# Recurrence gates as pairs of 64-row matmuls, joined by transfers, and a last output in halves

## The chip, the cores and the metric

The kernel runs on one core of a Trainium2 chip. The metric is the device time of one execution in microseconds (us). The engines are TensorE (PE, with its weight loads listed as PEld), VectorE (DVE), ScalarE (ACT), GpSimd (POOL) and SyncE (SP). Each works through its own queue in order. SP issues nearly all loads and stores, POOL a few.

## The reference, cut to what matters

One layer of an encoder over 512 tokens of 1024 features, in float32: a SwiGLU block, a mixer, a second SwiGLU block, each added to x. The mixer sums a gated linear recurrence (forward and backward) and a windowed attention. The change concerns the gates of the recurrence and the end of the second SwiGLU block:

```python
def _rglru_scan(xc, w_gates, b_gates, lam):          # called once for each direction
    xb = xc.reshape(B_, S, LRU_BLOCKS, LRU_BLOCK)    # 16 blocks of 64 features
    gates = jnp.einsum('bsni,gnio->gbsno', xb, w_gates)   # one 64x64 matrix per gate and block
    gates = gates.reshape(2, B_, S, W) + b_gates[:, None, None, :]
    r = jax.nn.sigmoid(gates[0])
    i = jax.nn.sigmoid(gates[1])
    log_a = -LRU_C * r * jax.nn.softplus(-lam)
    a = jnp.exp(log_a)
    bx = jnp.sqrt(-jnp.expm1(2.0 * log_a)) * (i * xc)
    _, h = lax.associative_scan(_lin_combine, (a, bx), axis=1)
    return h
...
xc = _centred_dwconv(xr, conv_w[l], conv_b[l])
y_lru = (h_fwd + h_bwd) * jax.nn.gelu(gr)
...
x = x + FFN_RES * _swiglu(_rmsnorm(x, norm_ffn2[l]), w_ffn2_gu[l], w_ffn2_down[l])   # the output
```

The gate matrices are block diagonal: a gate of 128 features is two independent 64x64 products.

## The kernel before, in words

Features lie on the 128 partitions, the 512 tokens along the free dimension; a "tile" f is 128 features x 512 tokens, so x has 8 tiles. Every float32 product is made of three matmuls on operands cut into a high and a low part: high x high, high x low, low x high (`mm3`, lines 144 to 147). `load_w` loads a weight chunk of up to 128x1024 through SP into one of three buffers `wraw` and cuts it into `wh` (a copy on ACT, L118) and `wl` (a subtraction on DVE, L121), four buffers each. A chunk of 1024 columns gives 24 matmuls over 512 tokens.

PSUM has two pools of four tiles of 128x512: `acc` for the large products, `aux` for the recurrence's gates, the attention and other small products. SBUF tiles of 128x512 come from a pool of 48 (`big_t`), pairs of them from a pool of four (`pair_t`).

The order on each queue is not written out by hand: a scheduler places each instruction by the program's order and its own estimates of durations, so that independent matmuls fill a wait. `after(i, prev)` adds an order by hand, `high_priority` puts evictions and weight cuts forward.

The stages, by the trace: first SwiGLU block to about 352 us; projection `xr` with the convolution, eight chunks, one per tile f; projections q, k, v for two halves of the heads, twelve chunks each (phases `t0`, `t1`); the gate branches, 24 chunks (`g`); the output projection; from about 800 us the second SwiGLU block, whose last products leave eight output tiles through `out2`.

The recurrence and the attention have no stage of their own. They are generators in two lanes, and after each chunk `weave(RATE[...])` runs some of their steps: for the recurrence four per chunk in `xr`, three in `t0`, two in `t1`, three in `g`. The recurrence's generator `lru(fs)` is entered twice, for tiles 0 to 3 once all four are convolved, and for tiles 4 to 7. For each tile it loads the gate matrices (128 x 512, zeros off the two diagonal blocks), cuts the convolved tile `xc` into `ch` and `cl`, and for each of two directions and two gates runs three matmuls of 128 rows (L145 to L147), evicts by a sigmoid on ACT (L606), multiplies the second gate by `xc` on DVE (L611) and takes a tanh of the first on ACT (L613). After four tiles come all exponentials (L618), all square roots (L623) and the scans on DVE (L631, L633); the groups stand together because ACT loads a table when the function changes.

In the second block's last products (`ffn`, from L416), the four outputs of a half are accumulated together until the last six of 22 steps k, which are run output by output; each output is then scaled (L442) and added to x (L901) on DVE and stored by SP (L902).

In the attention, `scores` (L744) already runs pairs of 64-row matmuls: for each of three products, one head on the upper and one on the lower 64 partitions, 256 columns each, into two PSUM tiles (L757).

Of the kernel before, what the change touches and what calls it, by code (L numbers as in the profile page):

```python
# [11 lines left out]
AF = mybir.ActivationFunctionType  # L12
ALU = mybir.AluOpType
# [3 lines left out]
P = 128  # L17
T = 512
# [49 lines left out]
def block_kernel(ctx: ExitStack, tc, a, out):  # L68
# [18 lines left out]
    def big_t(dt=F32, shape=(P, T), n="b"):  # L87
        return big.tile(list(shape), dt, tag="big", bufs=NBIG, name=nm(n))
# [7 lines left out]
    def aux_t():  # L96
        return aux.tile([P, T], F32, tag="aux", name=nm("aux"))
# [43 lines left out]
            split(raw[:, s], H[:, s], L[:, s], act)  # L141
        return H, L

    def mm3(ps, wh, wl, xh, xl, first, last):
        nc.tensor.matmul(ps, wh, xh, start=first, stop=False)  # L145
        nc.tensor.matmul(ps, wh, xl, start=False, stop=False)  # L146
        nc.tensor.matmul(ps, wl, xh, start=False, stop=last)  # L147

    def feat_chunk(src, nk, xh, xl, ps, k0, ktot, act=True):
        H, L = load_w(src, nk * P, act)  # L150
# [45 lines left out]
        nc.scalar.activation(r, ps, AF.Copy)  # L196
        return r, rcol, vx

    def after(i, prev):

        i, prev = getattr(i, "ins", i), getattr(prev, "ins", prev)
        tc.add_manual_dep(i, prev.name, mybir.DependencyInfo(
            mybir.DependencyClass.NoSync, mybir.DependencyReason.DATA), reason="order")


    mark = {}
# [127 lines left out]
    def ffn(wgu, ws, wd, xh, xl, S, ssum, plain, res, emit_out, lead=None):  # L334
        hs = []
        r = None
        pre = {}
# [78 lines left out]
        for q in range(2):  # L416
            outs = range(q * 4, q * 4 + 4)
            for i in range(2):
                t = pair_t()
                for m in range(2):  # L420
                    nc.sync.dma_start(t[:, m], res(q * 4 + i * 2 + m))
                    xres[q * 4 + i * 2 + m] = t[:, m]
            ps = [aux_t() if q == 0 else acc_t() for _ in outs]
            ws_ = []

            def put_in(i, k):
                H, L = ws_[k // 2]
                c = slice((k % 2) * T + i * P, (k % 2) * T + (i + 1) * P)
                mm3(ps[i], H[:, c], L[:, c], *cuts[q, k], k == 0, k == FT - 1)
# [8 lines left out]
            for i, m in enumerate(outs):  # L438
                for k in range(FT - 2 * DTAIL, FT):
                    put_in(i, k)  # L440
                t = big_t(n="dn")
                nc.vector.scalar_tensor_tensor(t, ps[i], -0.5, r, ALU.mult, ALU.mult)  # L442
                emit_out(m, t)


    lanes = {"lru": [], "att": []}
# [131 lines left out]
        xc[f] = y  # L578


    last_act = [None]

    def lru(fs):
        un = []
        cuts = {}

        def cut(f):
            if f in fs:
                cuts[f] = big_t(F32R, n="ch"), big_t(F32R, n="cl")
                split(xc[f], *cuts[f])  # L590

        cut(fs[0])
        for f in fs:
            gH, gL = load_w(a["wgate"][f], T)
            cut(f + 1)
            cH, cL = cuts.pop(f)
            yield
            for d in range(2):
                rt = []
                for g in range(2):  # L600
                    q = d * 2 + g
                    s = slice(q * P, (q + 1) * P)
                    ps = aux_t()
                    mm3(ps, gH[:, s], gL[:, s], cH, cL, True, True)
                    t = big_t(n="gate")
                    i = nc.scalar.activation(t, ps, AF.Sigmoid, bias=small[:, C_BG + f * 4 + q : C_BG + f * 4 + q + 1])  # L606
                    if last_act[0] is not None:
                        after(i, last_act[0])
                    rt.append(t)
                r, ix = rt  # L610
                nc.vector.tensor_tensor(ix, ix, xc[f], ALU.mult)  # L611
                th = big_t(n="th")
                tanh = nc.scalar.activation(th, r, AF.Tanh, scale=sp4[:, f * 2 + d : f * 2 + d + 1])  # L613
                un.append((f, d, r, ix, th))
                yield

        for f, d, r, ix, th in un:
            exp = nc.scalar.activation(r, r, AF.Exp, scale=sn8[:, f * 2 + d : f * 2 + d + 1])  # L618
            after(exp, tanh)
            nc.vector.scalar_tensor_tensor(ix, r, 1.0, ix, ALU.add, ALU.mult)  # L620
            yield
        for f, d, av, ix, th in un:
            last_act[0] = nc.scalar.activation(th, th, AF.Sqrt)  # L623
            after(last_act[0], exp)
            nc.vector.tensor_tensor(ix, ix, th, ALU.mult)
            yield
        h = None
        for f, d, av, ix, th in un:
            if d == 0:
                h = th  # L630
                nc.vector.tensor_tensor_scan(h, av, ix, 0.0, ALU.mult, ALU.add)  # L631
            else:
                nc.vector.tensor_tensor_scan(th[:, ::-1], av[:, ::-1], ix[:, ::-1], 0.0, ALU.mult, ALU.add)  # L633
                nc.vector.tensor_tensor(h, h, th, ALU.add)
                A[f] = h
            yield


# [14 lines left out]

    V = {}
# [246 lines left out]
        nc.vector.tensor_tensor(o, ps, xres[m], ALU.add)  # L901
        nc.sync.dma_start(out[m], o)  # L902

    ffn(a["w2gu"], a["w2s"], a["w2d"], xh, xl, forms.S, ssum, NPLAIN[1], lambda m: xd[m], out2)


def layouts(inp):
# [28 lines left out]
    bd = np.zeros((KT, P, 4, P), wg.dtype)  # L936
    for b in range(16):
        s = slice((b % 2) * 64, (b % 2) * 64 + 64)
        bd[b // 2, s, :, s] = wg[:, :, b].reshape(4, 64, 64).transpose(1, 0, 2)
    o["wgate"] = bd.reshape(KT, P, 4 * P)  # L940
    col = lambda v: np.asarray(v).reshape(-1, KT, P).transpose(2, 1, 0).reshape(P, -1)
    o["small"] = con(np.concatenate([
        col(f("norm_ffn1")[0]), col(f("norm_mix")[0]), col(f("norm_ffn2")[0]),
        col(f("conv_w")[0]), col(f("conv_b")[0]),
        col(f("lru_b_gates")[0].reshape(4, D)), col(f("lru_lambda")[0]),
        np.tile(f("q_norm")[0], 2)[:, None], np.tile(f("k_norm")[0], 2)[:, None]], 1))


# [31 lines left out]
```

## Time and profile before

| | |
|---|---|
| median of 3 runs | 1133.14 us (1133.12 to 1133.49) |
| the profiled execution | 1133.02 us, span of the program 1130.9 us |
| granted TensorE clock | 0.999 |
| TensorE matmuls | 6872, busy 1124.3 us (99%) |
| DVE, ACT, POOL busy | 836.0, 594.7 and 19.3 us |
| loaded from HBM, written | 121.17 MB, 8.39 MB |

The span runs from the first to the last instruction; 2.1 us of the execution lie around it. A row of a timeline gives start, duration, engine, line, operation, output<-inputs, shape and count; successive matmuls overlap in the pipeline, so their cost is the distance between starts. A row of grouped instructions ends with the busy time and mean duration in ns, then the idle time of the engine just ahead of them and what ended it. A row of waits gives who waited for whom, the sum in us, the count and the longest.

### The profile page before, as it was taken

Reading aid. Unit: us, or ns where it says so; the run is one execution under the profiler, and the core shown is the slowest. Engines: PE = TensorE matmul, PEld = TensorE weight load, DVE = VectorE, ACT = ScalarE, POOL = GpSimd, SP = SyncE. Lnnn points to the kernel's source line nnn. Section 1 sums busy time; section 2 is a strip of 40 time slices with the busy share of each in tenths; the row PEclk is TensorE's granted clock in tenths of the full one; section 3 lists DMA queues with packets and bytes.
Section 4 is the critical chain, followed back from the end, with each engine's and each line's share of the span. In section 5 each row is a group of like instructions: output and inputs, shape, how many; then the busy total and the mean of one; then the engine's idle time right before and its main releaser. Section 6 shows DMA issues by size and latency. Waiting matters only on the chain.

```text
span 1130.9 us, 17246 instructions
## 1 busy us (share of the span) xinstructions
PE 1124.3 (99%) x6872; PEld 995.1 (88%) x6872; DVE 836.0 (74%) x1288; ACT 594.7 (53%) x896; POOL 19.3 (2%) x52
## 2 busy tenths in 40 slices
PE   9999999999999999999999999999999999999998
PEld 8899999988888888888788888888999999998886
DVE  7898888884836798797855576859688888894542
ACT  8554544563624595985564254656445445464330
POOL 0000000000000000010110000000000000000000
PEclk9999999999999999999999999999999999999999
DMA  7242333443433342353443332355123233352320
GB/s 263 94 131 79 119 102 102 136 137 94 130 94 111 94 159 84 112 167 103 132 149 104 93 103 88 109 169 184 56 93 116 92 112 113 94 168 93 131 75 38
DMA packets 43553, 130.69 MB, mean 116 GB/s; under 512 B 5968, under 2 KB 8272, under 8 KB 43472
## 3 DMA queue, kind: packets, MB, share of 16 engines
q1 hardware_dynamic: 39600, 119.36, 33.8%
q0 software_dynamic: 3296, 9.97, 2.8%
q8 instruction: 54, 0.88, 0.3%
q10 hardware_dynamic: 576, 0.26, 0.1%
q14 instruction: 27, 0.22, 0.1%
HBM read 121.17 MB, written 8.39 MB: 115 GB/s over the span
## 4 chain that ended last, share of the span: by engine, by line
PE 97%; DVE 1%; ACT 1%; issue 0%; DVEq 0%
PE acc L260 29%; PE acc L145 11%; PE acc L146 11%; PE acc L147 11%; PE aux L260 5%; PE aux L145 4%; PE aux L146 4%; PE aux L147 4%; PE acc L666 4%; PE acc L665 3%; PE acc L667 3%; PE aux L784 1%; PE aux L795 1%; PE aux L757 1%; PE acc L373 1%; PE aux L373 0%
## 5 line engine op out<-in xcount | busy, mean ns | idle before, releaser
L118 ACT ACTIVATE wh<-wraw 128x1024 fp32r<-128x1024 f32 (+3 forms) x242 | 241.3, 999 | 333.9 <-PE acc L260 96.8
L121 DVE TENSOR_TENSOR wl<-wraw,wh 128x1024 fp32r<-128x1024 f32 (+3 forms) x254 | 291.4, 1150 | 138.5 <-ACT wh L118 137.9
L260 PE MATMUL acc<-s,wh 128*128 128x256 f32 x1216 | 220.6, 283 | 0.1
L260 PEld LDWEIGHTS acc<-s,wh 128*128 128x128 f32 x1216 | 189.7, 192 | 0.3 <-ACT p L317 0.3
L260 PE MATMUL acc<-s,wl 128*128 128x256 f32 x608 | 172.1, 283 | 0.0
L145 PE MATMUL acc<-xh,wh 128*128 128x512 f32 x304 | 120.2, 395 | 0.0
L146 PE MATMUL acc<-xl,wh 128*128 128x512 f32 x304 | 119.0, 392 | 0.0
L147 PE MATMUL acc<-xh,wl 128*128 128x512 f32 x304 | 118.8, 391 | 0.0
L260 PEld LDWEIGHTS acc<-s,wl 128*128 128x128 f32 x608 | 116.7, 192 | 0.0
L260 PE MATMUL acc<-xh,wl 128*128 128x256 f32 x304 | 86.0, 283 | 0.0
L260 PE MATMUL acc<-xl,wh 128*128 128x256 f32 x304 | 86.0, 283 | 0.0
L260 PE MATMUL acc<-xh,wh 128*128 128x256 f32 x304 | 86.0, 283 | 0.0
L665 PE MATMUL acc<-wh,xh 128*128 128x512 f32 x192 | 75.2, 392 | 0.0
L666 PE MATMUL acc<-wh,xl 128*128 128x512 f32 x192 | 74.8, 390 | 0.0
L667 PE MATMUL acc<-wl,xh 128*128 128x512 f32 x192 | 74.8, 389 | 0.0
L294 DVE TENSOR_TENSOR wraw<-wraw,pair 128x1024 f32<-128x1024 f32 x57 | 69.5, 1220 | 0.8
L145 PE MATMUL aux<-hh,wh 128*128 128x512 f32 x176 | 68.5, 389 | 0.0
L146 PE MATMUL aux<-hl,wh 128*128 128x512 f32 x176 | 68.5, 389 | 0.0
L147 PE MATMUL aux<-hh,wl 128*128 128x512 f32 x176 | 68.5, 389 | 0.0
L145 PE MATMUL acc<-hh,wh 128*128 128x512 f32 x176 | 68.5, 389 | 0.0
L146 PE MATMUL acc<-hl,wh 128*128 128x512 f32 x176 | 68.5, 389 | 0.0
L147 PE MATMUL acc<-hh,wl 128*128 128x512 f32 x176 | 68.5, 389 | 0.0
(194 smaller groups left out, 2197.5 us busy)
## 6 DMA issues: line engine op xcount, KB each, us to landing
wraw<-wqkv SPq DMA_DIRECT2D x24, 512.0 KB, 3.6
wraw<-wg SPq DMA_DIRECT2D x24, 512.0 KB, 3.6
wraw<-w1d SPq DMA_DIRECT2D x22, 512.0 KB, 3.6
wraw<-w2d SPq DMA_DIRECT2D x22, 512.0 KB, 3.6
pair<-w2s SPq DMA_DIRECT2D x20, 512.0 KB, 3.6
wraw<-w2s SPq DMA_DIRECT2D x20, 512.0 KB, 3.6
wraw<-w1s SPq DMA_DIRECT2D x18, 512.0 KB, 3.6
pair<-w1s SPq DMA_DIRECT2D x18, 512.0 KB, 3.6
```

The source lines that it names most:

```text
L118: nc.scalar.activation(H, raw, AF.Copy)
L121: nc.vector.tensor_tensor(L, raw, H.bitcast(F32), ALU.subtract)
L145: nc.tensor.matmul(ps, wh, xh, start=first, stop=False)
L146: nc.tensor.matmul(ps, wh, xl, start=False, stop=False)
L147: nc.tensor.matmul(ps, wl, xh, start=False, stop=last)
L260: nc.tensor.matmul(o, w_[:, c], x_, start=first and m + k == 0 and w_ is H and x_ is xh_, stop=m + k == 4 and w_ is L, skip_group_check=True)
L294: nc.vector.tensor_tensor(t, t, o, ALU.add)
L373: nc.tensor.matmul(pre[i], w[i][1][:, s], xh[k], start=k == 0, stop=False)
L665: nc.tensor.matmul(pss[j], xh[kk][:, tj], H[:, s], start=kk == 0, stop=False)
L666: nc.tensor.matmul(pss[j], xl[kk][:, tj], H[:, s], start=False, stop=False)
L667: nc.tensor.matmul(pss[j], xh[kk][:, tj], L[:, s], start=False, stop=kk == KT - 1)
L757: mm = nc.tensor.matmul(ps[hp][:, i * 256 : (i + 1) * 256], q_[o, n * P : (n + 1) * P], keys(k_[o]), start=k_ is kh and q_ is qh, stop=q_ ...
```

## The change

**Gates.** The gate matrices are stored without their zeros: 128 x 256, block b = 0 on partitions 0 to 63 and b = 1 on 64 to 127, with the columns of the two gates r and i of a direction side by side. A tile's products become 12 matmuls of 64 rows x 128 columns over 512 tokens, in six pairs (b = 0 and b = 1), into four `aux` tiles taken at once: one per direction and block, r on partitions 0 to 63 and i on 64 to 127. `after` chains the twelve, and the first of them waits, by a semaphore now, for the last sigmoid of the tile before. Four sigmoids evict into two `pair_t` tiles. Eight transfers per tile, each 64 partitions x 512 tokens, issued by POOL, put the two blocks of r together into one tile of 128 partitions, and those of i into another. The multiply by `xc` and the tanh (`use`) of a tile come during the next tile's steps.

**Steps.** There is one generator for all eight tiles, entered after tile 0's convolution instead of after tile 3's; a tile has six steps, of which the third holds its matmuls; the `xr` rate is three steps per chunk instead of four. Exponentials and square roots still come in two groups of four tiles, with a step for every two of them; the scans of the first four tiles are spread over the steps of the last four.

**Last output.** The last of the eight output tiles runs step k = 16 as before; for the last five k the products of the first 256 tokens come first, then those of the last 256, the latter into an `aux` tile. Scaling, adding and storing are done for each half.

```diff
-LRU_F = 4
+EHALF = 5
 RATE = {
-    "xr": {"lru": 4, "att": 0.0},
+    "xr": {"lru": 3, "att": 0.0},
...
+        def gates(f, W):
+            ps = [[aux_t() for _ in range(2)] for _ in range(2)]
+            X = cuts.pop(f)
+            mm = None
+            for d in range(2):
+                c = slice(d * P, (d + 1) * P)
+                for w, x in ((0, 1), (1, 0), (0, 0)):
+                    for b in range(2):
+                        o = slice(b * HD, (b + 1) * HD)
+                        prev, mm = mm, nc.tensor.matmul(
+                            ps[d][b], W[w][o, c], X[x][o], start=x == 1, stop=w + x == 0)
+                        if prev is not None:
+                            after(mm, prev)
+                        elif evicted:
+                            after(mm, evicted[-1], True)
+            for d in range(2):
+                q = C_BG + f * 4 + d * 2
+                both = pair_t()
+                for b in range(2):
+                    i = nc.scalar.activation(both[:, b], ps[d][b], AF.Sigmoid, bias=small[:, q + b : q + b + 1])
+                    if last is not None:
+                        after(i, last)
+                evicted.append(i)
+                r, ix = (big_t(n="gate") for _ in range(2))
+                for g, t in enumerate((r, ix)):
+                    for b in range(2):
+                        nc.gpsimd.dma_start(t[b * HD : (b + 1) * HD], both[g * HD : (g + 1) * HD, b])
+                got.append((f, d, r, ix))
+
+        def use():
+            f, d, r, ix = got.pop(0)
+            nc.vector.tensor_tensor(ix, ix, xc[f], ALU.mult)
+            th = big_t(n="th")
+            un.append((f, d, r, ix, th))
+            return nc.scalar.activation(th, r, AF.Tanh, scale=sp4[:, f * 2 + d : f * 2 + d + 1])
...
+            for f in fs:
+                W = load_w(a["wgate"][f], 2 * P)
+                early = len(got) > 0
+                for k in range(2):
+                    if early:
+                        tanh = use()
+                    yield
+                gates(f, W)
+                yield
+                cut(f + 1)
+                for _ in range(3):
+                    if todo:
+                        scan(*todo.pop(0))
+                    yield
...
     conv(f, ps, rb)
+        if f == 0:
+            lanes["lru"].append(lru())
     weave(RATE["xr"])
-        if (f + 1) % LRU_F == 0:
-            lanes["lru"].append(lru(range(f + 1 - LRU_F, f + 1)))
...
+        for k in range(k0, FT):
+            put_half(ps[i][:, t0], i, k, t0, False, k == FT - 1)
+        for k in range(k0, FT):
+            put_half(p2, i, k, t1, k == k0, k == FT - 1)
+        scaled(ps[i][:, t1], t1)
+        nc.vector.tensor_tensor(o[:, t1], t[:, t1], x[:, t1], ALU.add)
+        scaled(ps[i][:, t0], t0)
+        nc.vector.tensor_tensor(o[:, t0], t[:, t0], x[:, t0], ALU.add)
+        end(t0, o)
+        scaled(p2, t1)
+        nc.vector.tensor_tensor(o[:, t1], o[:, t1], t[:, t1], ALU.add)
+        end(t1, o)
```

More of the change, by code (lines that the diff above doesn't have):

```diff
@@ L142, in load_w, with mm3 @@
         return H, L
[L144 to L147, printed above, removed]
+    def mm3(ps, wh, wl, xh, xl, first, last, skip=False):
+        nc.tensor.matmul(ps, wh, xh, start=first, stop=False, skip_group_check=skip)
+        nc.tensor.matmul(ps, wh, xl, start=False, stop=False, skip_group_check=skip)
+        nc.tensor.matmul(ps, wl, xh, start=False, stop=last, skip_group_check=skip)
     def feat_chunk(src, nk, xh, xl, ps, k0, ktot, act=True):
@@ L332, in strassen, with ffn @@
         last_product(prev)
-    def ffn(wgu, ws, wd, xh, xl, S, ssum, plain, res, emit_out, lead=None):
+    def ffn(wgu, ws, wd, xh, xl, S, ssum, plain, res, emit_out, lead=None, end=None):
         hs = []
@@ L424, in ffn, with put_in, put_half @@
             ws_ = []
-            def put_in(i, k):
+            def put_in(i, k, last=FT - 1):
                 H, L = ws_[k // 2]
                 c = slice((k % 2) * T + i * P, (k % 2) * T + (i + 1) * P)
-                mm3(ps[i], H[:, c], L[:, c], *cuts[q, k], k == 0, k == FT - 1)
+                mm3(ps[i], H[:, c], L[:, c], *cuts[q, k], k == 0, k == last)
+            def put_half(o, i, k, tok, first, last):
+                H, L = ws_[k // 2]
+                c = slice((k % 2) * T + i * P, (k % 2) * T + (i + 1) * P)
+                mm3(o, H[:, c], L[:, c], *(t[:, tok] for t in cuts[q, k]), first, last, True)
             for j in range(FT // 2):
@@ L438, in ffn @@
             for i, m in enumerate(outs):
+                if end is not None and m == KT - 1:
+                    break
                 for k in range(FT - 2 * DTAIL, FT):
@@ L443, in ffn, with scaled @@
                 emit_out(m, t)
+        if end is None:
+            return
+        i, x, k0 = 3, xres[KT - 1], FT - EHALF
+        for k in range(FT - 2 * DTAIL, k0):
+            put_in(i, k, k0 - 1)
+        t, o, p2 = big_t(n="dn"), big_t(n="o"), aux_t()[:, :half]
+        t0, t1 = slice(0, half), slice(half, T)
+        def scaled(p, tok):
+            nc.vector.scalar_tensor_tensor(t[:, tok], p, -0.5, r[:, tok], ALU.mult, ALU.mult)
+        for k in range(k0, FT):
[10 more added lines that the diff above has]
+        end(t1, o)
     lanes = {"lru": [], "att": []}
@@ L578, in conv, with lru @@
         xc[f] = y
[L581 to L585, printed above, removed]
+    def lru():
+        got, evicted, cuts, last = [], [], {}, None
         def cut(f):
-            if f in fs:
+            if f < KT:
                 cuts[f] = big_t(F32R, n="ch"), big_t(F32R, n="cl")
                 split(xc[f], *cuts[f])
[L592 to L597, printed above, removed]
-            for d in range(2):
[L599 to L628, printed above, removed]
@@ L632, in lru @@
             else:
                 nc.vector.tensor_tensor_scan(th[:, ::-1], av[:, ::-1], ix[:, ::-1], 0.0, ALU.mult, ALU.add)
-                nc.vector.tensor_tensor(h, h, th, ALU.add)
-                A[f] = h
+                nc.vector.tensor_tensor(fwd[f], fwd[f], th, ALU.add)
+                A[f] = fwd[f]
+        fwd, todo = {}, []
+        cut(0)
+        for fs in (range(0, 4), range(4, 8)):
+            un = []
+            for f in fs:
[12 more added lines that the diff above has]
+                    yield
+            for _ in range(2):
+                tanh = use()
+                yield
+            for k, (f, d, r, ix, th) in enumerate(un):
+                exp = nc.scalar.activation(r, r, AF.Exp, scale=sn8[:, f * 2 + d : f * 2 + d + 1])
+                after(exp, tanh)
+                nc.vector.scalar_tensor_tensor(ix, r, 1.0, ix, ALU.add, ALU.mult)
+                if k % 2:
+                    yield
+            for k, (f, d, av, ix, th) in enumerate(un):
+                last = nc.scalar.activation(th, th, AF.Sqrt)
+                after(last, exp)
+                nc.vector.tensor_tensor(ix, ix, th, ALU.mult)
+                if k % 2:
+                    yield
+            todo += un
@@ L636, in lru @@
+        for t in todo:
+            scan(*t)
             yield
@@ L902, in out2 @@
         nc.sync.dma_start(out[m], o)
[L904 removed]
+    ffn(a["w2gu"], a["w2s"], a["w2d"], xh, xl, forms.S, ssum, NPLAIN[1], lambda m: xd[m], out2,
+        end=lambda tok, o: nc.sync.dma_start(out[KT - 1][:, tok], o[:, tok]))
 def layouts(inp):
@@ L935, in layouts @@
     wg = f("lru_w_gates")[0]
[L936 to L940, printed above, removed]
+    o["wgate"] = con(wg.reshape(2, 2, KT, 2, 64, 64).transpose(2, 3, 4, 0, 1, 5)).reshape(KT, P, 4 * 64)
     col = lambda v: np.asarray(v).reshape(-1, KT, P).transpose(2, 1, 0).reshape(P, -1)
+    bg = f("lru_b_gates")[0].reshape(2, 2, KT, 2, 64).transpose(1, 4, 2, 0, 3).reshape(P, 4 * KT)
     o["small"] = con(np.concatenate([
```

11 lines of the change are left out of this document (6 added, 5 removed).

## The prediction

> **What bounds the kernel now.** I read the page first: span, busy shares, and by engine the chain of work that ended last. TensorE holds 97% of the chain, so a microsecond taken from its queue is worth one, if nothing else ends later.
>
> ```profile
> span 1130.9 us, 17246 instructions
> PE   1124.3 (99%) x6872; PEld 995.1 (88%) x6872; DVE 836.0 (74%) x1288; ACT 594.7 (53%) x896; POOL 19.3 (2%) x52
> PE 97%; DVE 1%; ACT 1%; issue 0%; DVEq 0%
> ```
>
> Busy PE can be an overlap of modelled ends, so next comes the timeline of TensorE at the gates of one tile. What counts is the distance between starts.
>
> ```profile
> 389.84 0.39 PE L147 MATMUL acc<-xh,wl 128*128 128x512 f32 x1
> 390.07 0.39 PE L145 MATMUL aux<-ch,wh 128*128 128x512 f32 x1
> ...
> 392.56 0.39 PE L147 MATMUL aux<-ch,wl 128*128 128x512 f32 x1
> 392.79 0.39 PE L145 MATMUL acc<-xh,wh 128*128 128x512 f32 x1
> ```
>
> Twelve gate matmuls take 392.79 - 390.07 = 2.72 us, 0.227 us each, and the stream does not pause before or behind them. Then the stretches in which the recurrence runs, and in the last row the attention behind it (columns: time, and for PE, its weight loads, DVE, ACT and POOL the busy time and count; granted clock; DMA share; GB/s).
>
> ```profile
> 352.00:396.00 44.00, 44.00 (x200) 35.68 (x200) 32.42 (x47) 24.20 (x35) 0.66 (x10) 1.00 0.35 102
> 396.00:440.00 44.00, 44.00 (x196) 36.38 (x195) 41.52 (x55) 37.34 (x56) 2.42 (x6) 1.00 0.41 132
> 440.00:485.00 45.00, 45.00 (x200) 37.28 (x199) 32.27 (x50) 34.94 (x51) 1.28 (x2) 1.00 0.39 115
> 485.00:515.00 30.00, 30.00 (x134) 24.82 (x134) 29.49 (x39) 20.56 (x30) 3.01 (x5) 1.00 0.46 135
> 515.00:625.00 110.00, 109.42 (x683) 90.09 (x682) 72.62 (x183) 59.73 (x122) 8.96 (x15) 1.00 0.40 123
> ```
>
> DVE is nearly full in the second and fourth row (41.5 of 44, 29.5 of 30), yet TensorE stays at 44.00 and 30.00 there: the weights it needs are split early enough. The waits of 352 to 515 us say the same:
>
> ```profile
> ACT wh L118 <- PE acc L666: 22.1, 7, 4.8
> PEld aux L145 <- ACT ch L118: 0.4, 1, 0.4
> PEld aux L145 <- ACT gate L606: 0.4, 1, 0.4
> ```
>
> The split waits for TensorE to give a weight buffer back (22.1 us); TensorE's gate matmuls waited 0.8 us in all. So this stage is TensorE's.
>
> **The gate matmuls.** Removed are 8 tiles x 12 = 96 matmuls of 128 rows, in the list of the tile ch 32 of each of three kinds (high by high shown):
>
> ```profile
> L145 PE MATMUL aux<-ch,wh x32: 389/389/497, 384.0 to 479.4; 128*128 128x512 f32 x32
> ```
>
> 96 x 0.227 = 21.8 us. Added are 96 matmuls of 64 rows over 512 columns, in 48 pairs, one of each pair on the lower and one on the upper 64 partitions, into different PSUM tiles. No such size is in this trace. The attention scores are the nearest: 64 rows, 256 columns, the same six pairs.
>
> ```profile
> 531.67 0.39 PE L667 MATMUL acc<-wl,xh 128*128 128x512 f32 x1
> 531.99 0.39 PE L757 MATMUL aux<-kh,qh 64*128 64x256 f32 x2
> 532.21 0.28 PE L757 MATMUL aux<-kl,qh 64*128 64x256 f32 x2
> 532.33 0.28 PE L757 MATMUL aux<-kh,ql 64*128 64x256 f32 x2
> ...
> 532.69 0.28 PE L757 MATMUL aux<-kh,ql 64*128 64x256 f32 x2
> 532.90 1.09 PE L784 MATMUL aux<-ident,p 128*128 128x128 f32 x8
> 533.75 0.48 PE L665 MATMUL acc<-wh,xh 128*128 128x512 f32 x1
> 534.07 0.39 PE L666 MATMUL acc<-wh,xl 128*128 128x512 f32 x1
> ```
>
> A pair comes every 0.12 us, and a single 128-row matmul of 256 columns takes the same 0.12:
>
> ```profile
> 808.08 2.88 PE aux L260 x24
> ```
>
> (2.88 / 24). So the two halves of a pair run together, and a pair costs what one full matmul costs: at 512 columns 0.227 us. 48 x 0.227 = 10.9 us stay, 10.9 go. By a page of the Trainium skill, "TensorE: Matmul & The Clock Gate", section "Back-to-back issue gap", a sustained stream at 512 columns is said to run at about 131 ns a matmul; by that figure 96 matmuls are 12.6 us, 48 are 6.3, and 6.3 go instead of 10.9. The trace does not agree: every stream quoted here starts a matmul each 227 ns, so no chance is given to it.
>
> A run has a price at its ends. In these rows: 0.32 instead of 0.227 before the first pair (0.09), 0.22 instead of 0.12 behind it, since its weights could not be loaded ahead (0.10), 0.21 instead of 0.12 behind the last (0.09), and 0.32 instead of 0.227 for the first full matmul after a restart (0.09, after transposes here). Together 0.37 us. Eight runs: 3.0 us. The lower bound is 0.18 (first and third alone, the weight loads hiding under the wider pairs): 1.5 us. The upper is 0.74, each run broken once in two: 5.9 us. I take 3.0, the row's own sum. **Gates: 10.9 - 3.0 = 7.9 us gained, between 5.0 and 9.4.**
>
> **The wait ahead of a run.** Its first matmul now waits for the last sigmoid of the tile before. Everything behind it on TensorE's queue would stand too. Tiles are six steps apart, three steps to a chunk of 24 matmuls (24 x 0.227 = 5.4 us): 10.9 us. The tile's evictions are four sigmoids as before:
>
> ```profile
> L606 ACT ACTIVATE gate<-aux,small 128x512 f32<-128x512 f32 x32 | 20.7, 685 | 0.0
> L121 DVE TENSOR_TENSOR wl<-wraw,wh 128x512 fp32r<-128x512 f32 x8 | 5.5, 682 | 0.0
> ```
>
> 4 x 0.685 = 2.7 us of 10.9. Cost 0; its cover is 8 us of other ScalarE work per tile. The four PSUM tiles that a run takes at once are free by the same margin, and all eight runs end (the last at step 55 of the 60 before that point) ahead of the attention that shares them. Counts of sigmoid, tanh, exp, square root, multiply and scan do not change. The gate weights halve in width, so 8 loads and splits get cheaper (by at most 8 x 0.68 / 2 = 2.7 us on DVE, about as much on ACT); both engines are off the path: 0. The earlier start moves recurrence work into 352 to 396 us, where DVE has 11.6 us idle: 0.
>
> **The joins.** 64 transfers of 128 KB go on POOL's queue, eight a tile, four a direction. Their price is bounded by POOL's issues and landings now (columns of the last three: KB each, us to landing):
>
> ```profile
> 398.61 2.29 POOL L706 DMA_DIRECT2D bm<-rpb  x4 [0.45 <-issue]
> vd<-v POOLq DMA_DIRECT2D x8, 256.0 KB, 4.9
> bm<-rpb POOLq DMA_DIRECT2D x16, 384.0 KB, 5.0
> wraw<-wgate SPq DMA_DIRECT2D x8, 256.0 KB, 2.6
> ```
>
> 0.57 us an issue, 36 us on POOL in all, 4.6 of each 10.9. Behind them on POOL stand the memsets of the convolution's borders: late by a few us, they delay only a tile's own convolution, which is used a step later. Bytes: 8.4 MB in 87 us, 96 GB/s beside the 102 to 135 of the table above; the loads on SP have three buffers. What matters is who waits. Each multiply on DVE and tanh on ACT waits for its joined tiles in an in-order queue, with weight splits behind. By the steps, the first use comes four steps after the run, 7.3 us; the joined tile is there after two sigmoids (1.4), four issues (2.3) and 5.0 of landing: 8.7 us. Late by 1.4; the second direction, by POOL's order, at 1.4 + 8 x 0.57 + 5.0 = 11.0 against 9.1: 1.9. Sixteen uses, up to 26 us of standing on DVE and ACT. If all of it reached TensorE, 26 us are lost; if the landing is 2.6 as on SP's queue, none. The splits run ahead by whole chunks (the 22.1 us above), so I take 0.3 us.
>
> A row against a rule: the four issues at 398.61 took 0.57 us each while DVE was 94% busy. The Trainium skill, "SBUF — State Buffer", section "SBUF: two separate sides", says that a POOL transfer waits for its descriptors while DVE runs a copy or similar operation in a two-port mode. This row shows no such hold. By that rule, with each issue held for one DVE operation of 0.68, a use would come 2.7 us (first direction) or 5.4 us (second) later still. That is the first rival at a larger price; its chance holds this too.
>
> **The tail.** The last output now ends in halves.
>
> ```profile
> 1126.12 0.39 PE L147 MATMUL acc<-hh,wl 128*128 128x512 f32 x1
> 1126.55 0.69 DVE L442 SCALAR_TENSOR_TENSOR dn<-acc,rstd 128x512 f32<-128x512 f32 x1 [2.66 <-PE acc L147]
> 1127.27 0.69 DVE L901 TENSOR_TENSOR o<-dn,pair 128x512 f32<-128x512 f32 x1
> L211 DVE SCALAR_TENSOR_TENSOR s<-s,xg 128x256 f32<-128x256 f32 x16 | 6.7, 421 | 0.3
> L279 DVE TENSOR_TENSOR h<-s,p 128x256 f32<-128x256 f32 x38 | 15.5, 417 | 0.0
> out<-o SPq DMA_DIRECT2D x8, 256.0 KB, 2.0
> ```
>
> Removed: two operations of 0.69 behind the last matmul. Added there: two of 0.42: 0.54 us gained. TensorE does 30 matmuls of 0.12 for 15 of 0.227: 3.6 - 3.4, 0.2 lost. The four DVE operations for the other half (1.7 us) run beside the last 15 matmuls (1.8 us), just covered; without that cover up to 0.4 comes back. The last transfer is half as large: between 0 and 1.0 (a half of 256 KB's 2.0), I take 0.2. **Tail: 0.5 gained, between -0.1 and 1.3.**
>
> **Sum.** 7.9 + 0.5 - 0.3 = 8.1 us. The profiled execution took 1133.02 us (span 1130.9 and 2.1 around it), 0.1 under the median 1133.14. 1133.0 - 8.1 = **1124.9 us**.
>
> **Rivals.** (1) *The joined tiles come late and TensorE pays.* Place: DVE's multiply and ACT's tanh, with splits and PSUM evictions behind them; the token-row groups of the next projection take all four accumulators at once, so an eviction late by over 3 x 6 x 0.227 = 4.1 us stops TensorE. Price: up to 26 us. From 8.4 us on, a third of it, the kernel is slower; with half, 13 us, 1133.0 - 8.4 + 13 = 1137.6. Against it: the 22.1 us of lead. (2) *DVE becomes the bound in its full stretches*, by a smaller lateness: half of the gates' gain is lost, 1124.9 + 4 = 1129. For it, 41.5 of 44; against it, its total of 103 in 119 us, before 8 us go. (3) *The pairs take turns at 512 columns*: no matmul time is saved and 3.0 are paid, 1133.0 + 3.0 - 0.5 = 1135.5. Against it, 0.12 us a pair at 256. (4) *The gain is given back later*: attention's own chains set the pace behind 515 us and the start of attention does not move; 1132.5. Against it, TensorE's 109.4 of 110 us in the last row of the table of stretches: there too it is the busy one
>
> **Chances.** Forecast 0.78, by its own bounds 1122.3 (9.4 + 1.3) to 1128.1 (5.0 + 0.2 - 0.3); rival 1, 0.06; 2, 0.09; 3, 0.03; 4, 0.04. The range 1122.5 to 1129 takes in rival 2's value and cuts the rest. A measurement of this kernel tells 0.2% (2.3 us) from no change. Faster: the forecast and rival 2, 0.86. Same: rival 4 and a little of rival 1, 0.05. Slower: most of 1 and 3, 0.09.
>
> **What would show it.** Gate pairs 0.227 apart in runs of some 1.7 us, eight of them; 0.3 instead of 0.227 at a run's ends; TensorE at its full stretch from 352 to about 507 us; DVE's multiply and ACT's tanh waiting for the joined tiles by under 2 us each; the last two DVE operations at 0.42. Wrong if pairs start 0.45 apart, if gaps of over 1 us stand on TensorE between 360 and 500 with ACT or DVE waiting for a transfer, or if gate matmuls wait for a sigmoid.

## The result, and the profile after

The changed kernel takes 1142.49 us (median of 6 runs, 1140.32 to 1146.17) against 1133.21 of the kernel before on the same chip (1133.04 to 1133.49): a ratio of 1.0084, 95% interval 1.0073 to 1.0095. It is 9.3 us slower; 1124.9 was forecast, with a range of 1122.5 to 1129. The profiled execution took 1143.08 us.

The page of the changed kernel: span, TensorE's and the other engines' totals, chain by engine.

```profile
span 1141.3 us, 17452 instructions
...
PE 1124.6 (99%) x6887; PEld 989.1 (87%) x6887; DVE 834.0 (73%) x1292; ACT 591.9 (52%) x896; POOL 52.4 (5%) x116
...
PE 90%; ACT 3%; DVE 2%; issue 2%; DMA 2%; POOL 1%; ACTq 0%; DVEq 0%; POOLq 0%
```

TensorE's busy total is the same as before, to 0.3 us, and the chain has lost 7 points to ACT, DVE, DMA and POOL. That busy total misleads: matmuls at a lower clock count as longer (0.63 us instead of 0.39 in the rows at 400 us below). The stretches (the columns as before) show the place:

```profile
352.00:396.00 44.00, 43.07 (x206) 34.27 (x204) 23.73 (x36) 24.03 (x35) 8.80 (x22) 1.00 0.53 145
396.00:440.00 44.00, 38.43 (x165) 29.28 (x163) 36.49 (x53) 32.38 (x50) 10.84 (x26) 0.91 0.58 164
440.00:485.00 45.00, 44.51 (x205) 34.08 (x205) 35.40 (x53) 29.90 (x45) 12.36 (x24) 0.97 0.60 154
485.00:515.00 30.00, 27.42 (x113) 22.14 (x113) 20.02 (x26) 21.23 (x30) 8.37 (x15) 0.94 0.71 206
```

In each, TensorE stood full before; now it misses 0.9, 5.6, 0.5 and 2.6 us, and in three of them the granted clock is under 1.00. The gate runs themselves are as forecast. This is TensorE's timeline at one that nothing disturbed:

```profile
410.18 0.39 PE L146 MATMUL acc<-xl,wh 128*128 128x512 f32 x1
410.50 0.50 PE L632 MATMUL aux<-cl,wh 64*128 64x512 f32 x2
410.84 0.39 PE L632 MATMUL aux<-ch,wl 64*128 64x512 f32 x2
...
411.76 0.40 PE L632 MATMUL aux<-ch,wh 64*128 64x512 f32 x2
412.09 0.50 PE L147 MATMUL acc<-xh,wl 128*128 128x512 f32 x1
```

Pairs start 0.23 us apart and a run is 1.59 us long. Its ends: 0.32 instead of 0.227 ahead of it, 0.34 instead of 0.23 behind the first pair, 0.33 behind the last, and (not shown) 0.11 more at the first full matmul after it. Taken together the four ends cost 0.40 us a run; 0.37 was forecast. One of the eight runs is broken up by full matmuls (its pieces start at 435.79, 439.97 and 444.56, not shown).

The waits of 352 to 520 us:

```profile
DVE gate L655 <- DMA gate<-pair: 26.2, 10, 6.6
ACT th L658 <- DMA gate<-pair: 16.6, 8, 3.0
ACT wh L118 <- PE acc L736: 9.6, 4, 5.0
...
PEld aux L632 <- DVE cl L121: 7.2, 5, 4.2
...
PE aux L632 <- DVE cl L121: 5.2, 3, 3.8
```

Multiply and tanh stand 26.2 and 16.6 us for joined tiles. The lead of the weight copies (`wh` waiting for TensorE; before it was 26.5 us in this window, 22.1 up to 515 us) is down to 9.6. And TensorE, its weight loads 7.2 us and its matmuls 5.2 (in part the same stops), waits for `cl`: the cut of the *next* tile, made on DVE by line 121. On TensorE's timeline the stops of the four stretches are 5.2 us for `cl` (at 384.61, 400.01 and 483.20), 1.8 for an eviction of q and k on ACT (438.11) and 2.6 for one of v on DVE (493.13).

The list of the tile `gate` and the issues of weight loads, after:

```profile
L650 POOL DMA_DIRECT2D gate<-pair x64: 518/518/692, 372.0 to 493.1; - x64
...
DMA to landing us min/median/max: 2.2/5.2/7.3
```

```profile
wraw<-wqkv SPq DMA_DIRECT2D x24, 512.0 KB, 5.0
```

and the same load before:

```profile
wraw<-wqkv SPq DMA_DIRECT2D x24, 512.0 KB, 3.6
```

An issue on POOL takes 0.52 us, a landing 5.2 in the median and up to 7.3, and the 512 KB weight loads beside them have gone from 3.6 to 5.0 us. The chain in order of time shows how one late landing reaches TensorE (start, length, what):

```profile
384.61 1.65 PE aux L632 x12
...
387.77 0.96 POOL gate L650 x2
388.77 6.56 DMA gate<-pair
395.42 0.69 DVE gate L655
396.11 0.67 DVE xc L609
...
399.36 0.61 DVE cl L121
```

The run of one tile ends at 386.3; its joined tile lands at 395.3; the multiply, a weight split and pieces of the convolution, and the cut follow on DVE one after another, and only then can the run of the next tile start, at 400.01. DVE's own timeline says how long it stood there (in brackets the idle time ahead of the row):

```profile
395.42 0.69 DVE L655 TENSOR_TENSOR gate<-gate,xc 128x512 f32<-128x512 f32 x1 [6.55 <-DMA gate<-pair]
```

So from 388.87 on, for 6.55 us, with the convolution, a weight split and the cut behind it in its queue. On TensorE:

```profile
400.01 0.80 PE L632 MATMUL aux<-cl,wh 64*128 64x512 f32 x2 [3.75 <-DVE cl L121]
400.60 0.63 PE L632 MATMUL aux<-ch,wl 64*128 64x512 f32 x2
401.03 0.63 PE L632 MATMUL aux<-ch,wh 64*128 64x512 f32 x2
```

It stands for 3.75 us and then runs at half the rate: pairs are 0.43 apart instead of 0.23. The matmuls stay 0.43 apart until 405.17, five microseconds in all. The tail: two operations of 0.42 us behind the last matmul, as forecast.

```profile
1137.37 0.42 DVE L462 SCALAR_TENSOR_TENSOR dn<-aux,rstd 128x256 f32<-128x256 f32 x1 [0.37 <-PE aux L147]
1137.83 0.42 DVE L474 TENSOR_TENSOR o<-o,dn 128x256 f32<-128x256 f32 x1
```

### The profile page after: what moved, and what is told of

The parts are those of the page before. It is cut to its first block, busy times and chain, and to the rows that moved or that the text cites. A ratio compares the mean times of both kernels' runs of the same rounds, so it can differ in the third digit from the quotient of the medians.

```text
span 1141.3 us, 17452 instructions
## 1 busy us (share of the span) xinstructions
PE 1124.6 (99%) x6887; PEld 989.1 (87%) x6887; DVE 834.0 (73%) x1292; ACT 591.9 (52%) x896; POOL 52.4 (5%) x116
## 4 chain that ended last, share of the span: by engine, by line
PE 90%; ACT 3%; DVE 2%; issue 2%; DMA 2%; POOL 1%; ACTq 0%; DVEq 0%; POOLq 0%
PE acc L260 29%; PE acc L145 10%; PE acc L146 10%; PE acc L147 10%; PE aux L260 5%; PE aux L146 4%; PE aux L147 4%; PE aux L145 4%; PE acc L735 2%; PE acc L736 2%; DMA gate<-pair 2%; PE acc L737 2%; PE aux L854 1%; PE aux L865 1%; PE aux L827 1%
## 5 line engine op out<-in xcount | busy, mean ns | idle before, releaser
L735 PE MATMUL acc<-wh,xh 128*128 128x512 f32 x192 | 77.5, 404 | 4.4 <-DVE v L759 2.6
L145 PE MATMUL aux<-hh,wh 128*128 128x512 f32 (+1 forms) x181 | 69.9, 386 | 0.0
L146 PE MATMUL aux<-hl,wh 128*128 128x512 f32 (+1 forms) x181 | 69.9, 386 | 0.0
L147 PE MATMUL aux<-hh,wl 128*128 128x512 f32 (+1 forms) x181 | 69.9, 386 | 0.0
L147 PEld LDWEIGHTS acc<-xh,wl 128*128 128x128 f32 x304 | 57.4, 189 | 12.6 <-issue 0.7
L147 PE MATMUL acc<-hh,wl 128*128 128x512 f32 (+1 forms) x176 | 67.9, 386 | 0.0
L146 PE MATMUL acc<-hl,wh 128*128 128x512 f32 (+1 forms) x176 | 67.9, 386 | 0.0
```

What stands on the lines that cost most here:

```text
L145: nc.tensor.matmul(ps, wh, xh, start=first, stop=False, skip_group_check=skip)
L146: nc.tensor.matmul(ps, wh, xl, start=False, stop=False, skip_group_check=skip)
L147: nc.tensor.matmul(ps, wl, xh, start=False, stop=last, skip_group_check=skip)
L735: nc.tensor.matmul(pss[j], xh[kk][:, tj], H[:, s], start=kk == 0, stop=False)
```

## The experiments

Times are medians; the kernel before, run beside them, took 1133.2 to 1133.5 us. The edits are to the changed kernel unless said otherwise.

**1. No joins** (sigmoids write r and the second gate directly).

```diff
-both = pair_t()
...
+for b, t in enumerate((r, ix)):
+    i = nc.scalar.activation(t, ps[d][b], AF.Sigmoid, ...)
...
-        nc.gpsimd.dma_start(t[b * HD : (b + 1) * HD], both[g * HD : (g + 1) * HD, b])
```

> Leaves the joining out: the four sigmoids write two tiles that are used as r and i as they stand (blocks in the wrong places, the same amount of work), so no transfer and no wait for one. Theory A (the joined tiles land late, VectorE and ScalarE stand in their queues, and the cuts and evictions behind them stop TensorE): about 1125 us, TensorE without gaps over 1 us between 360 and 500. Theory B (the transfers' bytes and POOL's queue slow the weight loads): also about 1125. Theory C (the new order of steps, four PSUM tiles at once and the wait ahead of a run): 1138 to 1143, the gaps stay.

Measured: 1125.68 us, ratio 0.9935 (0.992 to 0.995). The stretches:

```profile
352.00:396.00 44.00, 43.79 (x213) 34.48 (x212) 32.92 (x49) 28.71 (x42) 0.66 (x10) 1.00 0.32 103
396.00:440.00 44.00, 44.00 (x204) 35.38 (x203) 41.38 (x57) 37.09 (x56) 2.42 (x6) 1.00 0.35 113
440.00:485.00 45.00, 45.00 (x213) 35.66 (x212) 31.77 (x49) 31.53 (x46) 3.06 (x5) 1.00 0.49 150
485.00:515.00 30.00, 30.00 (x138) 24.93 (x137) 28.05 (x37) 19.84 (x31) 1.20 (x2) 1.00 0.40 120
```

All but 0.2 us of TensorE's time is back, the clock is 1.00, and weight copies wait for TensorE 29.1 us in all (352 to 520 us). Matmuls in these four rows: 768, against 689 in the changed kernel; 79 x 0.227 = 17.9 us of work that the joins pushed out. TensorE's idle time in those rows accounts for 9.4 of it (9.6 against 0.2), the lower clock for most of the rest (0.09 x 44 + 0.03 x 45 + 0.06 x 30 = 7.1, at most, since TensorE also stood for a part of that time). The medians differ by 16.8. So the joins are 16.8 of the 17.6 us by which the forecast was off.

**2. The same transfers, read by nobody**; multiply into a separate tile.

```diff
+t = big_t(n="dump")
+nc.gpsimd.dma_start(t[b * HD : (b + 1) * HD], (r, ix)[b][g * HD : (g + 1) * HD])
```

> As the kernel without joins, but the 64 transfers of 128 KB run on POOL's queue into tiles that nobody reads: the same traffic, no use that waits. Theory A: within 2 us of the kernel without joins, about 1125. Theory B: 1135 to 1143, and the weight loads of the q, k, v projection stay at 5.0 us to landing. Theory C: 1138 to 1143.

Measured: 1136.1 us, ratio 1.0025 (1.0015 to 1.0034), 10.4 above experiment 1. Weight loads are as slow as in the changed kernel (5.0 us), and with nobody waiting for a join TensorE still lost time, among it one stop of 4.3 us, up to 438.59, for an eviction of q and k on ACT. ACT's timeline shows what that eviction stood behind, six square roots and not a join:

```profile
434.31 3.23 ACT L698 ACTIVATE th<-th 128x512 f32<-128x512 f32 x6
...
437.96 0.57 ACT L748 ACTIVATE qk<-acc 128x512 f32<-128x512 f32 x1
```

Taken alone, this run says that the bytes cost 10 us. Experiment 13 puts that right.

**3. 128-row gates in the new steps**, no joins: the order and the pacing of the change without its pairs.

```diff
-                            ps[d][b], W[w][o, c], X[x][o], ...
+                            ps[d][b], W[w][:, c], X[x], ...
```

> The changed steps, pacing wait, four PSUM tiles at once and the last output in halves, but the gates as twelve full matmuls of 128 rows on the zero-padded matrices, so no joins are needed. If pairs of 64 rows save what was forecast (7.9 us), this is 1132 to 1134, 7 to 9 us above the kernel without joins. Theory C: 1148 or more. If the pairs save nothing: the same as the kernel without joins.

Measured: 1133.36 us, ratio 1.0002 (0.9992 to 1.0011). The kernel before took 1133.24. This run has the output in halves too, worth 0.8 us by experiment 8, so the new steps cost some 0.9 us, within the intervals. The pairs save 1133.36 - 1125.68 = 7.7 us.

**4. Joined by the eviction**: eight sigmoids of 64 partitions, each writing where it belongs; no transfers.

```diff
+for g, t in enumerate((r, ix)):
+    i = nc.scalar.activation(t[b * HD : (b + 1) * HD], ps[d][b][h], AF.Sigmoid, bias=small[h, ...])
```

> Pairs of 64 rows, joined without transfers: eight sigmoids of 64 partitions instead of four of 128, each writing its half straight into r or i (two of four shift partitions). ScalarE does 32 x 0.68 = 22 us more in a stage where it has about 40 idle. Theory A: 1125 to 1128, no waits for a transfer. Theory B: the same. If ScalarE becomes the bound: 1130 to 1136. Theory C: 1138 or more.

Measured: 1135.18 us, ratio 1.0017 (1.0007 to 1.0026). In the second stretch ACT is now the full one, 42.4 of 44 us, 37.3 before.

**5. As 2, with a quarter of the bytes** (128 of 512 tokens).

> As the kernel with transfers that nobody reads (1136.1 us), with a quarter of each: 64 partitions x 128 tokens instead of 512. POOL issues the same 64 transfers at the same places. If the bytes beside the weight loads are what still costs 10 us there: 1126 to 1129, and the loads of the q, k, v weights land in 3.6 to 4.2 us. If POOL's queue, the waits of its issues, or the order that the scheduler makes of it is the cost: 1133 to 1137.

Measured: 1127.15 us, ratio 0.9947 (0.9933 to 0.9961). The number of transfers and POOL's issues are the same, so neither is the price. Bytes and time to land changed together (a median of 3.7 us to landing, against 5.6 in 2).

**6. Uses two tiles later** in the program, where the change has them one tile later.

```diff
-early = len(got) > 0
+early = len(got) > 2
```

> The changed kernel, with the joined tiles used two tiles later instead of one (another 10 us). If the 43 us that VectorE and ScalarE stood for landings are the larger part: 1127 to 1132. If the traffic beside the weight loads is the larger part, the waits vanish from the list and the time stays at 1135 to 1138, near the kernel with unread transfers.

Measured: 1134.11 us (1132.78 to 1139.49), ratio 1.0011 (1.0001 to 1.0021): 8.4 better than the change. Neither of the two expectations came true: DVE's waits are still there.

```profile
DVE gate L655 <- DMA gate<-pair: 17.9, 10, 5.1
```

A later step in the program is not a later place on DVE: the scheduler orders each queue by its own estimates, and its order of multiplies and cuts is still the one of the change (a multiply at 393.91, the next cut at 395.19); the first multiply starts at 378.75, in the change at 378.82. TensorE's stops for `cl` are no shorter (0.91, 3.12, 1.13 and 1.73 us). ACT's waits for joins are gone, TensorE stands 7.1 us in the four stretches instead of 9.6, and the granted clock is 1.00 in all four: most of the 8.4 us is the clock.

**7. Joins by POOL copies** instead of transfers.

```diff
-nc.gpsimd.dma_start(t[...], both[...])
+nc.gpsimd.tensor_copy(t[...], both[...])
```

> The changed kernel with the 64 transfers replaced by 64 copies on POOL itself, 64 partitions each, half of them to the other half of the partitions: no bytes on the DMA engines, the result joined all the same. If landing and traffic are the cause, and a copy takes 1 us or less: 1126 to 1130, and the list of waits shows no transfer of gates. If POOL's copies hold VectorE up or take over 1.3 us each (more than 10.9 us a tile): 1135 or more.

Measured: 1139.2 us, ratio 1.005 (1.0034 to 1.0066). Minimum, median and maximum in the list of the tile:

```profile
L650 POOL COPY gate<-pair x64: 604/958/1589, 371.9 to 492.9; 64x512 f32<-64x512 f32 x64
L655 DVE TENSOR_TENSOR gate<-gate,xc x16: 677/692/1092, 376.0 to 493.6; 128x512 f32<-128x512 f32 x16
```

A copy takes 0.96 us and up to 1.59; and DVE's operations beside them stretch, a multiply from 0.69 to 1.09. The Trainium skill, "SBUF — State Buffer", section "SBUF: two separate sides", says that a DVE operation with two SBUF inputs and a GpSimd operation that reads SBUF exclude each other; these rows agree.

**8. The tail alone**, on the kernel before.

> The kernel before with the last output in halves alone. Forecast's term: 0.5 us faster, 1132.6 to 1132.8; the last two VectorE operations take 0.42 us each. If the half transfer lands no sooner and the 30 short matmuls cost more than 0.2: no change.

Measured: 1132.54 us, ratio 0.9993 (0.9984 to 1.0002): 0.8 us in the medians.

**9. Uses behind the next tile's cut**, by hand; the transfers stay.

```diff
+after(t, cutins[f + 1][0])      # tanh behind ch on ACT
+after(m, cutins[f + 1][1])      # multiply behind cl on DVE
```

> The changed kernel with two orders by hand: a tile's multiply on VectorE and its tanh on ScalarE stand behind the cut of the next tile, which TensorE's next run needs. The transfers stay. If TensorE's gaps at the gates come from the cut standing behind a multiply that waits for a landing, the gaps of 1 to 4 us ahead of a run go and what is left is the traffic: 1133 to 1137, as with the unread transfers (1136.1) or a little less. If traffic is all: 1140 to 1143.

Measured: 1132.37 us (1130.89 to 1135.15), ratio 0.9993 (0.9984 to 1.0003): 10.1 better than the change, with all its bytes.

```profile
ACT th L659 <- DMA gate<-pair: 17.5, 7, 4.7
DVE gate L656 <- DMA gate<-pair: 16.4, 6, 5.0
...
PEld acc L740 <- ACT qk L753: 3.5, 4, 2.3
```

The waits for joins are 34 us in all, against 43, but what stood behind them has changed: TensorE's waits for `cl` are down to 2.3 and 1.1 us, and it now stops behind the evictions of q, k and v. TensorE stands 4.8 us in the four stretches instead of 9.6, and the granted clock is 1.00 in all of them, so a part of the 10.1 us is the clock.

**10. Joins issued by ScalarE's queue.**

> The changed kernel with the 64 transfers issued by ScalarE right behind its sigmoids instead of by POOL. Same bytes, no POOL queue. If POOL's issue and landing (5.2 us) are what made the uses wait: landings of 2 to 3 us, 1130 to 1136. If the bytes beside the weight loads set the landing: still 4 to 6 us, 1137 to 1143, and 64 issues on ScalarE more.

Measured: 1157.06 us, ratio 1.0211 (1.0197 to 1.0225), slower than either expectation.

Away from POOL's queue the landing is 4.4 us in the median instead of 5.2, hardly better, and 64 issues of 0.54 us (up to 1.27) now stand in the queue of the engine that evicts. TensorE's two longest stops, 6.1 and 5.5 us, are for evictions of q and k on ACT. The Trainium skill, "SBUF — State Buffer", section "SBUF: two separate sides", advises this move, off POOL's queue, where VectorE holds up POOL's descriptors. The issues on POOL showed no such hold (0.518 in the minimum and in the median), and the move made it worse.

**11 to 14.** Two more with the eight half sigmoids: every second weight copy of two stages on DVE (11), and entered after tile 2 with the old rate (12). Then the two edits of 6 and 9 together (13), and 11 with the order of 9 (14).

```diff
+            k = min(f + 2, max(cutins))     # 13: behind the cut two tiles on,
+            if k > f:                       #     and len(got) > 2 as in 6
+                after(t, cutins[k][0])
+                after(m, cutins[k][1])
```

> The kernel with eight half sigmoids and no transfers (1135.2 us), with every second weight copy of the xr and of the first q, k, v chunks on VectorE instead of ScalarE (0.69 instead of 1.06 us). If ScalarE's 22 us of added sigmoids cost it its gain: 1127 to 1131. If the order of the steps is the cause: 1134 to 1136.

> The kernel with eight half sigmoids and no transfers (1135.2 us), with the recurrence entered after tile 2 instead of tile 0 and four steps per chunk. If TensorE's gaps there come from runs that stand close behind their own tile's convolution and cut: 1127 to 1131, no gap over 1 us ahead of a run before 410 us. If ScalarE is the bound: 1133 to 1137.

> The changed kernel, its joined tiles used two tiles later and behind the cut of the tile that TensorE needs next. All transfers stay. If standing for landings is what is left of the loss in the run with the order by hand (1132.4 us): waits for gate transfers under 5 us in all and 1126 to 1129. If the bytes beside the weight loads are: 1130 to 1134.

> The kernel with eight half sigmoids, no transfers and weight copies shared with VectorE (1132.0 us), with the multiply and the tanh behind the next tile's cut. If its gaps of 1.8 to 2.3 us ahead of runs come from the cut standing behind them: 1127 to 1130. If they come from ScalarE's load: 1131 to 1133.

| | us | ratio, 95% interval |
|---|---|---|
| 11 | 1131.96 | 0.9989 (0.998 to 0.9998) |
| 12 | 1136.2 | 1.0023 (1.0014 to 1.0031) |
| 13 | 1126.74 | 0.9944 (0.9932 to 0.9957) |
| 14 | 1134.43 | 1.001 (1.0001 to 1.0019) |

Relieving ACT brings the half sigmoids to 1.3 us under the kernel before, no more (the first expectation of 11 was missed by 1 us); a later entry doesn't help, and 14 missed its expectation. Why the order that helps the transfers hurts there is open.

Number 13 is faster than both kernels. On DVE the cut comes ahead of the multiply now; then the waits and the second stretch:

```profile
389.13 0.68 DVE L620 TENSOR_TENSOR cl<-xc,ch 128x512 fp32r<-128x512 f32 x1
...
394.41 0.69 DVE L656 TENSOR_TENSOR gate<-gate,xc 128x512 f32<-128x512 f32 x1
```

```profile
ACT wh L118 <- PE acc L742: 26.3, 9, 4.4
...
DVE gate L656 <- DMA gate<-pair: 3.3, 2, 3.2
```

```profile
396.00:440.00 44.00, 44.00 (x204) 35.42 (x203) 42.71 (x60) 37.46 (x58) 12.65 (x29) 1.00 0.66 186
```

Every transfer is still there, and still lands after 3.9 us in the median and 7.8 at the latest; multiply and tanh wait 3.3 us instead of 43, the lead is 26.3 us (26.5 before), and TensorE is full in the stretch in which it lost most. It is 1.1 us above experiment 1: in this order the bytes and their landings cost about that.

**15. Short landings, read**: a quarter of the bytes as in 5, in the program's order of the change, with multiply and tanh waiting for them.

```diff
+nc.gpsimd.dma_start(t[b * HD : (b + 1) * HD, :P], ones[g * HD : (g + 1) * HD])
```

> The changed kernel with the sigmoids writing the two gate tiles directly, and the 64 transfers cut to a quarter of their bytes (64 partitions x 128 tokens, of a constant) into those same tiles, so that multiply and tanh still wait for a landing, in the same place and order. Left out: a quarter of each gate tile is overwritten by the constant, and the 64-row blocks stay where the matmuls put them. If the standing as such costs the time, however short the landing: 1134 to 1140, with waits of multiply and tanh summing to over 30 us. If it is the length of the landing that pushes a wait past what the lead covers (the prediction's own condition, 2.6 us to landing costs nothing): landings under 4 us in the median, waits under 20 us in sum, 1126 to 1130.

Measured: 1126.17 us, ratio 0.9936 (0.9918 to 0.9954).

```profile
DVE gate L653 <- DMA gate<-ones: 8.8, 7, 3.0
...
ACT th L656 <- DMA gate<-ones: 4.9, 4, 2.0
```

With landings of 2.9 us in the median (4.4 at the latest), multiply and tanh still wait 13.7 us in all, 3.0 at the longest, and nothing reaches TensorE. But the order on DVE had not stayed. In the change the cut of tile 1 comes behind both multiplies of tile 0, and the cuts of tiles 2 and 3 behind the first multiply of the tile before; here tile 1's comes behind one multiply, and those of 2 and 3 ahead of both. So landing and order changed together, and two more runs hold the order.

**16 and 17. Cuts behind the first multiply of the tile before**, by hand, for every tile but 0 and 4: 16 with the transfers of 15, 17 with those of the change.

```diff
+if behind is not None:          # in cut
+    after(cl, behind)
...
 tanh = use()
+if k == 0:
+    cut(f, mults[-1])
...
-cut(f + 1)
+if f == 3:
+    cut(4)
```

> As e15b (a quarter of the bytes, read; a quarter of each gate tile overwritten by a constant, 64-row blocks left where the matmuls put them), but every cut of a tile is held behind the first multiply of the tile before, by hand, so that the order on VectorE is the one that hurt in the changed kernel. If the length of the landing decides: 1126 to 1130, as e15b. If a cut behind a waiting multiply costs even with landings of 3 us: 1133 to 1140, with TensorE waiting for the cut.

> The changed kernel, nothing left out, with the same hold as e16: the control. By either theory as slow as the changed kernel or slower, 1139 to 1148. If it comes out under 1135, holding the cut behind the multiply changes more of the order than meant, and e16 tells nothing.

Measured: 16, 1132.29 us, ratio 0.9994 (0.9984 to 1.0004); 17, 1146.26 us, ratio 1.0109 (1.0091 to 1.0127). Waits of 16, then of 17:

```profile
DVE gate L656 <- DMA gate<-ones: 8.2, 5, 2.5
...
PEld acc L739 <- ACT qk L752: 4.0, 2, 2.0
```

```profile
DVE gate L658 <- DMA gate<-pair: 32.8, 10, 7.2
...
PEld aux L635 <- DVE cl L620: 10.8, 5, 3.5
```

| | a quarter of the bytes | all bytes |
|---|---|---|
| cut not held back by a join | 1126.17 (15) | 1126.74 (13) |
| cut behind the multiply | 1132.29 (16) | 1146.26 (17) |

With the cut held back, full transfers instead of quarters cost 14.0 us; without, 0.6, though 13 and 15 differ in more than the bytes (13 has its uses a tile later). Bytes and time to land change together here (a median of 3.4 us to landing in 16, 5.0 in 17); no run parts the two. The 0.6 holds for the orders of 13 and 15 alone: 2 and 5, in which nobody waits, differ by 9.0 us, and in 2 an eviction had come to stand behind the square roots. The hold costs 6.1 us even with short landings (weight loads stand 4.0 us behind evictions of q and k, and only 1.2 us of matmul waits are for `cl`), and 19.5 with full ones. 16 came out between its two expectations, so both length and order count; 17 is as slow as expected.

## Why the prediction was wrong, by its own steps

**Gates, 7.9 us: held.** 7.7 by experiments 3 and 1. The pairs overlap at 512 columns, which rules out rival 3, and the ends cost 0.40 a run.

**The wait ahead of a run, 0: held.** No row shows a gate matmul waiting for a sigmoid, and the steps without pairs and joins cost under 1 us, within the intervals (experiment 3).

**Tail, 0.5: held.** 0.8 by experiment 8, whose interval takes in both and zero. A slip in the sum: the forecast's upper bound, 1128.1, takes 0.2 for the tail where its own lower bound was -0.1 (1128.4); nothing hangs on it.

**The joins, 0.3 us: this step failed.** They cost 16.8 (1142.49 - 1125.68). Three parts of it were wrong, one was right in the main. The prediction's own sign of being wrong came, a gap of over 1 us on TensorE with DVE waiting for a transfer.

The landing was right in the median, 5.2 us for 5.0, and for the first run: 8.7 us after the start of the run were summed for the first direction, and the first run starts at 370.06 and its multiply at 378.82, 8.8 us later. It was too short for others: the run shown above starts at 384.61 and its tile lands 10.7 us later, with a landing of 6.56. The issues took 0.52 instead of 0.57, and the rule on descriptors, weighed there as a larger price, had no part in it.

*"By the steps, the first use comes four steps after the run, 7.3 us."* A step is a place in the program and not a time. DVE reached that multiply 4.3 us after the run had begun (388.87 against 384.61), where a scheduler that goes by its own estimates had put it. So a use stood up to 6.6 us and not 1.4 or 1.9. The prediction's 26 us, the lateness of sixteen uses added up, was met on DVE (26.2), but in ten waits, and ACT stood 16.6 beside it, 42.8 in all. Experiment 6 shows it from the other side: two tiles later in the program, DVE's waits only fell from 26.2 to 17.9.

*"The splits run ahead by whole chunks (the 22.1 us above), so I take 0.3 us."* The lead of the weight splits was looked up, and other work behind the same wait was not. In DVE's queue stood the rest of the convolution and the cut of the next tile, which has no such lead: the next run waits for it. Experiment 9 puts the cut ahead of the uses and gets 10 us back; 17 holds it behind them by hand and is 3.8 us slower than the change. The evictions of q, k and v came next, where rival 1 had put them (4.1 us of slack): 4.4 of TensorE's 9.6 us in the change, the longest stops that are left in experiment 9 (1.9 and 1.6 us), and the one of 4.3 us in experiment 2. The eviction of v that stopped TensorE in the change stood on DVE behind two multiplies that had waited 1.96 us each and two weight splits. Those of q and k, there and in experiment 2, stood on ACT behind a row of square roots, in 2 with nobody waiting for a join.

*The bytes beside the loads*, "96 GB/s beside the 102 to 135", were taken as free. Weight loads beside them went from 3.6 to 5.0 us in the change, though experiments 6 and 13, with the same transfers, have 3.8 and 4.5. With all bytes a held-back cut costs 14.0 us more than with a quarter (17 against 16), and with a cut that is not held back 0.6 (13 against 15).

On top came what no step had: after its three longest stops (3.75, 2.58 and 1.82 us) TensorE runs at half rate for 3 to 5 us, at most 7.1 of the 16.8 us.

**The rivals.** Number 1, given 0.06, is what happened in mechanism: the joined tiles come late and TensorE pays. Its place, the evictions, holds for 4.4 us of TensorE's stops; 5.2 were the cut. It was turned down by one row, the 22.1 us, which speaks for one kind of work. Its price, up to 26 us, was an upper bound on standing; 26.2 and 16.6 us of standing on two engines became 16.8 us of the kernel's time. Rival 2 (DVE as the bound) did not come: in experiment 13 DVE is busy 42.7 of 44 us in the second stretch and TensorE is full. Rival 4 did not come either: with the joins out of the way (1) or harmless (13) the gain stays to the end.

## What to carry to other kernels

When a change puts a wait on an in-order queue, list everything behind it up to the next thing that the bottleneck engine needs, and take the smallest lead among them, not that of the most frequent one. Distance in the program is not distance in time if a scheduler orders the queues: place a consumer behind a named instruction, as experiment 13 does, which keeps all of the change and takes 1126.74 us. To separate a transfer's price into issue, bytes with landing, and order, vary one at a time; the transfers that nobody read (2) pointed at the bytes, and only the table of 13, 15, 16 and 17 showed that bytes with their landing cost about 1 us in one order and 14 in the other.

## What the runs showed of the hardware

A stop of 3.75 us on TensorE is followed by pairs 0.43 instead of 0.23 us apart. From the start of that run to its sixth full matmul, at 405.17, are 5.16 us, and 2.85 in the undisturbed run at 410.50, so the stop costs over half as much again. The Trainium skill, "TensorE: Matmul & The Clock Gate", section "Part 1: The HAM clock gate", says that the clock halves after an idle window of about 3.4 us and comes back after a busy one; the rows at 400 us agree, with half rate for 5.2 us. Other rows show that the length of a stop alone does not tell: half rate also sets in 0.8 to 1.3 us after shorter stops in the change, of 1.82 us (ended at 438.11) and of 2.58,

```profile
493.13 0.50 PE L735 MATMUL acc<-wh,xh 128*128 128x512 f32 x1 [2.58 <-DVE v L759]
...
494.35 0.63 PE L736 MATMUL acc<-wh,xl 128*128 128x512 f32 x1
```

and does not follow one of 3.12 us in experiment 6:

```profile
395.93 0.50 PE L632 MATMUL aux<-cl,wh 64*128 64x512 f32 x2 [3.12 <-DVE cl L121]
396.26 0.40 PE L632 MATMUL aux<-ch,wl 64*128 64x512 f32 x2
```

What decides there was not tested.

Transfers of 128 KB from SBUF to SBUF land in 2.2 us at best and 7.3 at worst in the change (9.4 in experiment 2). The 512 KB loads beside them take 5.0 us in the median there instead of 3.6, but 3.8 in experiment 6. A quarter of the bytes lands in 2.9 us in the median (experiment 15). Beside copies on POOL a multiply on DVE goes from 0.69 to as much as 1.09 us.
